# One layer of a pool/S5/ConvFFN decoder on one core: sums and loads queued behind paced instructions, a norm split by tile, pieces of 512 columns

## The chip, the cores and the metric

The kernel runs as one launch on 1 core of a Trainium2 chip. The metric is device time in microseconds, the median of 3 runs. TensorE is called PE here, VectorE DVE, ScalarE ACT, GpSimd POOL, SyncE SP. Each of these engines takes its instructions in the order in which they stand in its own queue; semaphores hold an instruction until the data that it needs, or the buffer that it writes, is there. Everything behind a held instruction on that engine waits too, the DMAs that SP and POOL start among it.

## The reference

2072 tokens (16 meta tokens and 2048 prompt tokens as one sequence, and 8 single sample tokens) pass through one layer of width 1024. Cut to its core:

```python
h = rmsnorm(x, norm1_g)
u_pool, u_ssm, g_pool, g_ssm = split(h @ w_in)            # 512, 512, 1024, 1024 columns
y_pool = pool_mixer(u_pool)                                # windowed means minus the token, then 128 -> 256 per group
y_ssm  = glu_out(ssm_mixer(u_ssm), w_glu)                  # 32 groups, complex diagonal scan
x = x + (sigmoid(g_pool) * y_pool + sigmoid(g_ssm) * y_ssm) @ w_out
h2 = rmsnorm(x, norm2_g)
g, v = split(h2 @ w_up)                                    # 2816 columns each
x = x + (gelu(conv_b + causal_conv3(g, conv_w)) * v) @ w_down
y = rmsnorm(x, norm_f_g)
```

The outputs are y for prompt and sample tokens, and the new pool, SSM and convolution states of both. All is float32.

## The kernel before

**Products.** A float32 operand is split into a high part, rounded by ACT (L126), and a low part, the rest, which DVE (or POOL) subtracts (L127). Each product is three matmuls, high by high, high by low, low by high (`mm3`, L145 to L147).

**First stage, tokens as columns.** The tokens are cut into six `PIECES` of 280, 384, 384, 384, 384 and 256 columns. `norm_piece(j)` loads tiles of 128 tokens (`xt`, four buffers, all by SP), takes the mean square on ACT, the inverse root in a dozen tiny DVE instructions (`rsqrt`, L175 to L186), scales (L260) and transposes on PE (`ptr_n`, L195). Part 0 of the work is pieces 0 and 1, part 1 the others. Eight tiles of `w_in` give u (`pu`, `pp`), then the gates (`pgs`, `pg`, and `py` for the pool map), 24 weight tiles in all, each over every piece: 8 contraction steps of three matmuls a piece. The results go through three buffers tagged `ev` (`us`, `up`, `sg`, `gs`). Before the results of piece 0 are put in, POOL clears a margin of the buffer (L283, L306), and so waits there until the buffer is free.

**Sums of w_up.** `pre_sums` (L325 to L340) prepares sums of blocks of `w_up` for the Strassen-like products below: 22 units, each four POOL-started loads of 128 KB, four POOL instructions, one POOL-started store of 512 KB to `WS`, in two buffers `pre`. They are taken through the loop over the first products, and beside the gates of part 0.

**SSM.** `ssm_setup` builds tables on DVE, which POOL copies (`TSt`, `TCt`, L596, L597); then come the SSM steps, between which gate units of part 1 are put.

**Output product and second norm.** `out_products(j)` multiplies by `w_out` into `po` and adds to x (L1048), tile by tile; `out_norm(j)` does `rsqrt` for all tiles of the piece at once, scales (`xs`, L1066) and transposes (`pn`, L1072), and the result goes to H2 in DRAM.

**Up stage.** Three superblocks s of columns. `b_tiles(s)` loads four tiles of H2 (688 KB each, SP, L1096) and forms four sums: POOL's L1105, L1106, L1123 (L1119 for s > 0), DVE's L1117. Each of the seven operands is split into x. Then 22 steps f, each with seven weight operands made by `w_ops` (loads by SP, high part ACT, low part DVE), each times x in 12 matmuls of 344 columns (`puX`, `puY`, `puZ`). The down product follows (`pd`, 512 columns).

**The order** on each engine is not the program text's: a scheduler with its own time estimates places instructions, within the data dependences and `tc.issue_after`, which keeps an instruction behind another one in the order.

Of the kernel before, what the change touches and what calls it, by code (L numbers as in the profile page):

```python
# [9 lines left out]
F32 = mybir.dt.float32  # L10
F32R = mybir.dt.float32r
# [23 lines left out]

PIECES = [(0, 280), (280, 664), (664, 1048), (1048, 1432), (1432, 1816), (1816, 2072)]
PARTS = [(0, 1), (2, 3, 4, 5)]
SKIP = 14
# [25 lines left out]
def hybrid_kernel(ctx, tc, x_prompt, x_sample, state_pool, state_re, state_im, state_conv, meta,  # L64
# [209 lines left out]
    def u_ssm(m, j, w):  # L274

        a, b = PIECES[j]
        n = b - a
        ps = bank("A", f"pu_{m}_{j}")
        proj(ps, w, j)
        us = evac.tile([P, TC * 50], F32, tag="ev", name=f"us_{m}_{j}", bufs=3)  # L280
        if j == 0:
            u = us.rearrange("p (t c) -> p t c", t=TC)
            GP.memset(u[:, :, 0:16], 0.0)  # L283
            V.tensor_copy(u[:, 7, 0:8], ps[:, 14:22])
            V.tensor_copy(u[:, 0, 8:16], ps[:, 14:22])
# [12 lines left out]
    def u_pool(m, j, w):
# [3 lines left out]
        proj(ps, w, j)  # L302
        up = evac.tile([P, TC * 50], F32, tag="ev", name=f"up_{m}_{j}", bufs=3)
        rows = UP[m * P:(m + 1) * P, :]
        if j == 0:
            GP.memset(up[:, 0:16], 0.0)  # L306
            V.tensor_copy(up[:, 16:30], ps[:, 0:14])
# [8 lines left out]
        else:  # L316
            S.copy(up[:, 0:n], ps[:, 0:n])
            dma(rows[:, 16 + a - 8:16 + b - 8], up[:, 0:n])
            if j == 5:
                pq = bank("B", f"pl_{m}")  # L320
                T.transpose(pq[0:15, 0:P], up[:, n - 15:n], ident)
                V.tensor_copy(psamp[0:15, m * P:(m + 1) * P], pq[0:15, 0:P])
                if m == 3:
                    dma(pool_p[0, 0], psamp[0:15, :])
# [23 lines left out]
    for n, (i, j) in enumerate([(0, 0), (1, 0), (0, 1), (1, 1)] + [(i, j) for i in range(2, 8) for j in PARTS[0]]):  # L348
# [3 lines left out]
        (u_ssm if m >= 4 else u_pool)(m % 4, j, u_w[i])  # L352
        if n in (1, 5, 9, 13):
            norm_piece(2 + n // 4)
        if n >= 6:
            next(pre_units)
    with tc.issue_after(w_ins[0]):
# [36 lines left out]
    def pool_d(g, j):  # L394
# [4 lines left out]
        n = b - a if j else 258  # L399
        ut = gpool.tile([P, 400], F32, tag="ut", name=f"ut_{g}_{j}_{len(hT)}", bufs=2)  # L400
        dma(ut[:, 0:n + 16], UP[g * P:(g + 1) * P, pos0:pos0 + 16 + n])
        cur = ut
        step = 1
        while step < w:
            nxt = gpool.tile([P, 400], F32, tag=f"s{step % 3}", name=f"s_{g}_{j}_{step}", bufs=1)
            lo = 2 * step - 1
            V.tensor_tensor(nxt[:, lo:n + 16], cur[:, lo:n + 16], cur[:, lo - step:n + 16 - step], op=ADD)
            cur = nxt
            step *= 2
        d = gpool.tile([P, 384], F32, tag="d", name=f"d_{g}_{j}", bufs=1)  # L410
        dh = gpool.tile([P, 384], F32R, tag="dh", name=f"dh_{g}_{j}", bufs=2)
        dl = gpool.tile([P, 384], F32R, tag="dl", name=f"dl_{g}_{j}", bufs=2)
        o = 0 if j else NS
# [9 lines left out]
    def gate_pool(g, part):  # L423
# [7 lines left out]
        for j in PARTS[part]:  # L431
# [3 lines left out]
            for i in range(2):  # L435
# [4 lines left out]
                mm3(py[:, 0:n], ph[:, i * P:(i + 1) * P], pl[:, i * P:(i + 1) * P], dh[:, 0:n], dl[:, 0:n], True, True)  # L440
                sg = evac.tile([P, TC * 50], F32, tag="ev", name=f"sg_{m}_{j}", bufs=3)
                S.activation(sg[:, 0:n], ps[:, 0:n], AF.Sigmoid)
# [5 lines left out]
    def gate_ssm(m, part):  # L448
        w = w_in_tile(16 + m, f"gs{part}_{m}")
        for j in PARTS[part]:  # L450
# [4 lines left out]
            proj(ps, w, j, skip)  # L455
            sg = evac.tile([P, TC * 50], F32, tag="ev", name=f"gs_{m}_{j}", bufs=3)
            S.activation(sg[:, 0:n], ps[:, 0:n], AF.Sigmoid)
# [360 lines left out]
    n_steps, done = G + len(STAGES) - 1, 0  # L818
    SSM_END = 68
    units = gate_units()  # L820
# [176 lines left out]
    def out_products(j):  # L997
# [32 lines left out]
        for t, (o, r, p0) in enumerate(tiles):  # L1030
# [19 lines left out]
            jk = osc.tile([P, D], BF16, tag="junk", name=f"ojk_{j}_{t}", bufs=1)  # L1050
            S.activation(jk[0:r], xt[0:r], AF.Square, accum_out=ss[0:r, t:t + 1])
        return ss, rs, x2

    def out_norm(j, ss, rs, x2):
        a = GP_PIECES[j][0]
        tiles = col_tiles(j)
        if j == 0:
            with tc.issue_after(stores[-1]):
# [3 lines left out]
            gdma(H2v[:, :, 0:NU - NG], zpad)  # L1062
        rsqrt(osc, rs[:, 0:len(tiles)], ss[:, 0:len(tiles)], len(tiles), f"n2_{j}")
        for t, (o, r, p0) in enumerate(tiles):
            xs = ost.tile([P, D], F32, tag="xs", name=f"xs_{j}_{t}", bufs=1)
# [19 lines left out]
    asamp = upA.tile([P, NF, NS], F32, name="asamp")  # L1085

    def b_tiles(s):

# [6 lines left out]
        for dst, k0, c in ((b11, 0, c0), (b12, 0, c0 + NH), (b22, 4, c0 + NH), (b21, 4, c0)):  # L1095
            dma(dst, H2v[:, k0:k0 + 4, c:c + NH])  # L1096
        ops = {}
# [9 lines left out]
        if s == 0:  # L1107

            t2 = ot.tile([P, 4 * NH + P], F32, name="t2")[:, P:].rearrange("p (k c) -> p k c", k=4)
            GP.tensor_tensor(t2, b22, t, op=SUB)  # L1110

        def make(key):
            if key in ops:
                return ops[key]
            if key == 6:
                if s:
                    V.tensor_tensor(b11, b22, t, op=SUB)  # L1117
            if key == 4 and s:
                GP.tensor_tensor(b11, b21, b11, op=SUB)  # L1119
            sp(key, {1: b11, 6: b11 if s else t2, 7: b12, 5: t, 3: b22, 4: b11, 2: b21}[key])  # L1120
            return ops[key]

        make.last = lambda: GP.tensor_tensor(b11, b21, t2, op=SUB)  # L1123
        return make
# [3 lines left out]
    def w_ops(s, f):  # L1128
# [4 lines left out]
        st = upA.tile([P, 3, 4, P], F32, tag="st", name=f"ws_{s}_{f}", bufs=2)  # L1133
        later(r1, w_up[:, f * P:(f + 1) * P].rearrange("(k p) c -> p k c", p=P))
        value = w_up[:, DFF + f * P:DFF + (f + 1) * P].rearrange("(k p) c -> p k c", p=P)
        ops = {}

        def sp(key, src):
            if (s, f) == (0, 0) and key in ORDER[:3]:
                hi, lo = [fw0.tile([P, 4, P], F32R, name=f"w{n}0_{key}") for n in "hl"]  # L1140
            else:
                made[0] += 1
                pl, n = (fw, 6) if made[0] % 9 < 6 else (fw2, 3)
                hi = pl.tile([P, 4, P], F32R, tag="wh", name=f"wh{key}_{s}_{f}", bufs=n)
# [180 lines left out]
    lctx = ExitStack()  # L1325
    xc = lctx.enter_context(pool("xc"))
    with tc.high_priority(offset=120):
        for key in ORDER[:3]:
            mk(key)
        mk.last()  # L1330
    pctx.close()
# [273 lines left out]
```

## Time and profile before

| | us |
|---|---|
| median of 3 runs | 2455.31 (2452.75 to 2457.64) |
| profiled execution, whole | 2457.64 |
| its span | 2455.7 |
| PE busy | 2376.1 (97%) |
| DVE busy | 1660.0 (68%) |
| POOL busy | 1036.7 (42%) |
| ACT busy | 983.2 (40%) |

The table is read as follows. The profiled execution is the slowest of the three runs, and 1.9 us of it lie around the span. PE is the engine with next to no slack: 79.6 us of the span are without a matmul. What a change is worth is therefore read from where PE stands idle, and from the length of its queue. The other engines' shares are means over stages that differ much, so the views by stretch are of more use than the means. The stages by time: first norm and u products of part 0 to about 114 us; gates of part 0 to 238; tables of the SSM and u of part 1 to 300; SSM steps with gates to 640; rest of the gates and the GLU to 890; output product and second norm to 1080; up stage to 1990; down stage to the end.

### The profile page before, as it was taken

What the parts mean: (1) busy time and instruction counts of PE and PEld (TensorE: products, weight loads), DVE (VectorE), ACT (ScalarE), POOL (GpSimd) and SP (SyncE); (2) the same over time, 40 slices, a digit from 0 to 9 for tenths busy, and PEclk for the clock granted to TensorE, in tenths of its full rate; (3) what the DMA queues carried; (4) which work ended last, traced back from release to release, by engine and by line L of the source; (5) the groups of instructions that cost most, each with busy time, mean ns of one, the idle gap of its engine ahead of it and who ended that gap; (6) DMA issues with size and microseconds to landing.
All of it is one profiled execution on the core that took longest, in us unless ns stands there. A gap on an engine that the chain in (4) does not pass through costs nothing. (4 is left out here: it accounts for less than half of the span.)

```text
span 2455.7 us, 38129 instructions
## 1 busy us (share of the span) xinstructions
PE 2376.1 (97%) x13628; PEld 2217.1 (90%) x13628; DVE 1660.0 (68%) x2916; ACT 983.2 (40%) x1814; POOL 1036.7 (42%) x1343
## 2 busy tenths in 40 slices
PE   6899999999999999989999999999999999999997
PEld 5899989999999988869999999999999987877876
DVE  6635868997566333468888987778776764555776
ACT  4422222222243122245555655556555543322433
POOL 6676178887113220114565642334333313331373
PEclk9999999999999999999999999999999999999999
DMA  8986543434467576655656665555565577645673
GB/s 250 246 252 205 95 126 104 119 100 116 117 178 222 148 225 192 197 162 169 202 181 203 210 210 182 183 196 170 188 202 172 178 245 265 206 154 168 211 249 125
DMA packets 433137, 449.45 MB, mean 183 GB/s; under 512 B 91372, under 2 KB 349288, under 8 KB 432931
## 3 DMA queue, kind: packets, MB, share of 16 engines
q1 hardware_dynamic: 389091, 353.89, 47.9%
q0 software_dynamic: 18512, 63.48, 7.9%
q10 hardware_dynamic: 25344, 29.66, 3.4%
q8 instruction: 107, 1.75, 0.3%
q14 instruction: 83, 0.68, 0.1%
HBM read 317.38 MB, written 129.86 MB: 182 GB/s over the span
## 5 line engine op out<-in xcount | busy, mean ns | idle before, releaser
L145 PE MATMUL puX<-x,wh 128*128 128x344 f32 x1056 | 337.8, 323 | 6.1 <-ACT u L1201 4.3
L146 PE MATMUL puX<-x,wh 128*128 128x344 f32 x1056 | 339.5, 322 | 1.1 <-DVE x L127 1.1
L147 PE MATMUL puX<-x,wl 128*128 128x344 f32 x1056 | 336.2, 320 | 0.0
L1525 PE MATMUL pd<-th,sl 128*128 128x512 f32 x600 | 235.2, 394 | 4.5 <-DVE sl L127 4.5
L1523 PE MATMUL pd<-th,sh 128*128 128x512 f32 x600 | 234.8, 394 | 3.0 <-ACT th L126 2.0
L1524 PE MATMUL pd<-tl,sh 128*128 128x512 f32 x600 | 236.9, 395 | 0.6 <-DVE tl L127 0.6
L126 ACT CAST wh<-wr 128x512 fp32r<-128x512 f32 x264 | 163.1, 619 | 164.9 <-PE puX L146 99.6
L127 DVE TENSOR_TENSOR wl<-wr,wh 128x512 fp32r<-128x512 f32 x264 | 202.1, 770 | 31.2 <-ACT wh L126 30.8
L1298 POOL TENSOR_TENSOR tr<-tr,tr 128x512 f32<-128x512 f32 x77 | 114.0, 1482 | 243.3 <-DMA tr<-in_w_down_dram 235.7
L127 DVE TENSOR_TENSOR sl<-sr,sh 128x512 fp32r<-128x512 f32 x154 | 133.6, 900 | 121.2 <-ACT sh L126 117.7
L145 PEld LDWEIGHTS puX<-x,wh 128*128 128x128 f32 x1056 | 198.8, 189 | 7.4 <-ACT u L1201 5.2
L127 DVE TENSOR_TENSOR wl<-ws,wh 128x512 fp32r<-128x512 f32 x198 | 168.4, 853 | 52.2 <-ACT wh L126 52.0
L146 PEld LDWEIGHTS puX<-x,wh 128*128 128x128 f32 x1056 | 199.3, 189 | 1.5 <-DVE x L127 1.4
L147 PEld LDWEIGHTS puX<-x,wl 128*128 128x128 f32 x1056 | 199.0, 189 | 0.0
L145 PE MATMUL puZ<-x,wh 128*128 128x344 f32 x528 | 170.3, 323 | 0.0
L146 PE MATMUL puZ<-x,wh 128*128 128x344 f32 x528 | 169.8, 322 | 0.0
L147 PE MATMUL puZ<-x,wl 128*128 128x344 f32 x528 | 168.7, 319 | 0.1
L126 ACT CAST wh<-ws 128x512 fp32r<-128x512 f32 x198 | 122.5, 619 | 109.4 <-PE puX L146 78.2
L126 ACT CAST sh<-sr 128x512 fp32r<-128x512 f32 x154 | 88.1, 617 | 177.9 <-PE pd L1524 159.6
L1523 PEld LDWEIGHTS pd<-th,sh 128*128 128x128 f32 x600 | 113.2, 189 | 31.2 <-ACT th L126 2.5
L1525 PEld LDWEIGHTS pd<-th,sl 128*128 128x128 f32 x600 | 113.1, 189 | 30.8 <-DVE sl L127 5.8
L1524 PEld LDWEIGHTS pd<-tl,sh 128*128 128x128 f32 x600 | 113.3, 189 | 25.6 <-DVE tl L127 1.0
(538 smaller groups left out, 6778.5 us busy)
## 6 DMA issues: line engine op xcount, KB each, us to landing
ws<-WS SPq DMA_DIRECT2D x55, 768.0 KB
wr<-in_w_up_dram SPq DMA_DIRECT2D x77, 512.0 KB
tr<-in_w_down_dram SPq DMA_DIRECT2D x150, 256.0 KB
sr<-SD SPq DMA_DIRECT2D x70, 512.0 KB
SD<-c POOLq DMA_DIRECT2D x44, 344.0 KB, 3.5
wr<-WS SPq DMA_DIRECT2D x55, 256.0 KB
wr<-in_w_up_dram SPq DMA_DIRECT2D x55, 256.0 KB
SD<-e POOLq DMA_DIRECT2D x22, 516.0 KB, 6.8
```

The source lines that it names most:

```text
L126: S.copy(hi, raw)
L127: return (eng or V).tensor_tensor(lo, raw, hi.bitcast(F32), op=SUB)
L145: T.matmul(ps, wh, xh, start=start, stop=False, **kw)
L146: T.matmul(ps, wh, xl, start=False, stop=False, **kw)
L147: T.matmul(ps, wl, xh, start=False, stop=stop, **kw)
L1298: GP.tensor_tensor(raws[0], raws[0], raws[n + 1], op=op)
L1523: T.matmul(acc[j], xh[:, c], th, start=k == 0, stop=False)
L1524: T.matmul(acc[j], xh[:, c], tl, start=False, stop=False)
L1525: T.matmul(acc[j], xl[:, c], th, start=False, stop=k == NP - 1)
```

## The change

There are five parts.

1. The last three pieces of 384, 384 and 256 columns become two of 512. The `ev` buffers and the pool mixer's buffers grow, `d` shares the buffers of the running sums, and gate units of part 1 are spread to step 51 where it was 68, there being fewer of them.
2. A unit of `pre_sums` in the first loop is placed behind the last margin clearing on POOL (`begin[0]`, L283 or L306). The x tiles of later pieces are loaded after n = 1, 5 and 9, pieces of 512 tokens being four tiles.
3. The H2 loads of superblocks 1 and 2 are placed behind the weight load of step f = 12 of the superblock ahead of them (`middle`).
4. `out_norm` takes a range of tiles. The last piece's tile 0 is normed inside `out_products(5)`, tile 1 after the first up products, each with its own `rsqrt` of one column.
5. The pool `fm` is opened earlier, weight operands are shared out 5 and 4 over the two pools where it was 6 and 3, and the sum for key 4 of superblock 0 goes from POOL (`make.last`, L1123) to DVE, at the place where key 4 is made (L1127 after).

```diff
-PIECES = [(0, 280), (280, 664), (664, 1048), (1048, 1432), (1432, 1816), (1816, 2072)]
-PARTS = [(0, 1), (2, 3, 4, 5)]
+PIECES = [(0, 280), (280, 664), (664, 1048), (1048, 1560), (1560, 2072)]
+PARTS = [(0, 1), (2, 3, 4)]
...
-            GP.memset(u[:, :, 0:16], 0.0)
+            begin[0] = GP.memset(u[:, :, 0:16], 0.0).ins
...
-            GP.memset(up[:, 0:16], 0.0)
+            begin[0] = GP.memset(up[:, 0:16], 0.0).ins
...
-        if n in (1, 5, 9, 13):
+        if n in (1, 5, 9):
             norm_piece(2 + n // 4)
         if n >= 6:
-            next(pre_units)
+            with tc.issue_after(begin[0]):
+                next(pre_units)
...
-        d = gpool.tile([P, 384], F32, tag="d", name=f"d_{g}_{j}", bufs=1)
+        d = gpool.tile([P, 528], F32, tag=f"s{step % 3}", name=f"d_{g}_{j}", bufs=1)
...
-    SSM_END = 68
+    SSM_END = 51
...
+            if (j, t) == (5, 0):
+                out_norm(j, ss, rs, x2, (0, 1))
...
-        rsqrt(osc, rs[:, 0:len(tiles)], ss[:, 0:len(tiles)], len(tiles), f"n2_{j}")
-        for t, (o, r, p0) in enumerate(tiles):
+        rsqrt(osc, rs[:, t0:t1], ss[:, t0:t1], t1 - t0, f"n2_{j}_{t0}")
+        for t, (o, r, p0) in list(enumerate(tiles))[t0:t1]:
...
-            dma(dst, H2v[:, k0:k0 + 4, c:c + NH])
+            with tc.issue_after(middle[-1]) if s else nullcontext():
+                dma(dst, H2v[:, k0:k0 + 4, c:c + NH])
...
-            if key == 4 and s:
-                GP.tensor_tensor(b11, b21, b11, op=SUB)
+            if key == 4:
+                (GP if s else V).tensor_tensor(b11, b21, b11 if s else t2, op=SUB)
...
-        make.last = lambda: GP.tensor_tensor(b11, b21, t2, op=SUB)
...
-        later(r1, w_up[:, f * P:(f + 1) * P].rearrange("(k p) c -> p k c", p=P))
+        ins = later(r1, w_up[:, f * P:(f + 1) * P].rearrange("(k p) c -> p k c", p=P)).ins
+        if f == 12:
+            middle.append(ins)
...
-                pl, n = (fw, 6) if made[0] % 9 < 6 else (fw2, 3)
+                pl, n = (fw, 5) if made[0] % 9 < 5 else (fw2, 4)
...
-        mk.last()
...
-    out_norm(5, *rest)
+    out_norm(5, *rest, (1, 2))
```

Three places show how the instructions move. On POOL, at the start of the kernel before (`pre_0`, `pre_1` are the first two units of sums, `us_0` the first buffers to be cleared, `wlo_u` the low parts of the first two weight tiles):

```order
L283 MEMSET us_0_348 128x8x16
L283 MEMSET us_0_382 128x8x16
L334 DMA pre_0_713<-in_w_up_dram 128x2x128
masks.py:199 ISA
masks.py:199 AFFINE_SELECT ident<-ident 128x128
L334 DMA pre_0_713<-in_w_up_dram 128x2x128 x3
L334 DMA pre_1_751<-in_w_up_dram 128x2x128 x4
L127 TENSOR_TENSOR wlo_u_4_234<-raw_u_4_232,whi_u_4_233 128x1024
L335 TENSOR_TENSOR pre_0_713<-pre_0_713 128x256
L127 TENSOR_TENSOR wlo_u_5_240<-raw_u_5_238,whi_u_5_239 128x1024
```

The same place of the changed kernel:

```order
L283 MEMSET us_0_346 128x8x16
L283 MEMSET us_0_380 128x8x16
masks.py:199 ISA
masks.py:199 AFFINE_SELECT ident<-ident 128x128
L127 TENSOR_TENSOR wlo_u_4_232<-raw_u_4_230,whi_u_4_231 128x1024
L127 TENSOR_TENSOR wlo_u_5_238<-raw_u_5_236,whi_u_5_237 128x1024
L283 MEMSET us_0_555 128x8x16
L283 MEMSET us_0_722 128x8x16
L334 DMA pre_0_731<-in_w_up_dram 128x2x128 x4
L334 DMA pre_1_769<-in_w_up_dram 128x2x128 x4
L306 MEMSET up_0_810 128x16
```

The first load of the sums has moved behind the fourth clearing of a buffer; the fourth clearing of an `up` buffer comes 21 rows further on, when three and a half units are through.

On DVE, at the second norm's last piece before (`xs_0` and `xs_1` are its two scaled tiles, `ri_n`, `rt_n`, `ors` belong to its `rsqrt`, `wl` is the low part of a weight operand):

```order
L186 SCALAR_TENSOR_TENSOR ri_n_5_11954<-rt_n_5_11953,ri_n_5_11954 128x2
L1237 SCALAR_TENSOR_TENSOR c_0_12093<-stT,colv,c_0_12093 128x8
L184 TENSOR_TENSOR rt_n_5_11953<-ri_n_5_11954 128x2
L185 TENSOR_TENSOR rt_n_5_11953<-rt_n_5_11953,rh_n_5_11952 128x2
L186 SCALAR_TENSOR_TENSOR ors_11759<-rt_n_5_11953,ri_n_5_11954 128x2
L1066 SCALAR_TENSOR_TENSOR xs_0_11968<-x_5_0_11766,ors_11759,g2B 128x1024
L127 TENSOR_TENSOR wl_0_1_12129<-wr_0_1_11748,wh_0_1_12128 128x512
L127 TENSOR_TENSOR wl_0_2_12255<-wr_0_2_12247,wh_0_2_12254 128x512
L1066 SCALAR_TENSOR_TENSOR xs_1_11984<-x_5_1_11774,ors_11759,g2B 128x1024
```

And in the changed kernel, where the first of the two stands, with the up stage's first operands (`x_0`) behind it and the sum that was POOL's:

```order
L1050 TENSOR_TENSOR x_5_1_10989<-po_1_0_11076,x_5_1_10989 128x512
L1071 SCALAR_TENSOR_TENSOR xs_2_10934<-x_4_2_10773,ors_10695,g2B 128x1024
L1050 TENSOR_TENSOR x_5_1_10989<-po_1_1_11077,x_5_1_10989 128x512
L1071 SCALAR_TENSOR_TENSOR xs_0_11060<-x_5_0_10981,ors_10974,g2B 128x1024
L127 TENSOR_TENSOR x_0_11139<-b_0_10674,x_0_11139 128x1376
L127 TENSOR_TENSOR x_0_11142<-bt_10678,x_0_11142 128x1376
L1127 TENSOR_TENSOR b_0_10674<-b_0_10675,t_10685 128x1376
L127 TENSOR_TENSOR x_0_11152<-b_0_10675,x_0_11152 128x1376
```

`xs_0` has moved ahead of all splits of the first superblock; `xs_1` follows 28 rows after the rows shown.

On SP, the H2 loads of superblock 1 (`b_1`) before, among the last stores to H2 and the weights of step 2 (`wr_0_2`, `ws_2`):

```order
L1049 DMA X2D<-x_5_1_11774 128x1024
L1096 DMA b_1_15367<-H_79 128x4x344
L1096 DMA b_1_15369<-H_79 128x4x344
L995 DMA wr_0_2_12247<-in_w_up_dram 128x8x128
L1096 DMA b_1_15370<-H_79 128x4x344
L1081 DMA H_79<-ht_2_11721 128x8x128
L1096 DMA b_1_15368<-H_79 128x4x344
L995 DMA ws_2_12249<-WS 128x1536
```

And after the change, among the weights of steps 11 to 13:

```order
L997 DMA wr_0_12_13033<-in_w_up_dram 128x8x128
L1104 DMA b_1_14593<-H_79 128x4x344
L997 DMA WS<-ws_11_12881 128x1536
L1104 DMA b_1_14595<-H_79 128x4x344
L997 DMA ws_12_13035<-WS 128x1536
L1104 DMA b_1_14596<-H_79 128x4x344
L1104 DMA b_1_14594<-H_79 128x4x344
L997 DMA wr_0_12_13034<-WS 128x512
```

The four loads have moved ten weight steps down the queue, and POOL's two sums of them with it.

## Rows read from the trace of the kernel before

**Rows 1.** By stretch: PE, PEld, DVE, ACT, POOL busy, clock, DMA, GB/s.

```profile
0.00:24.00 24.00, 5.82 (x27) 4.78 (x28) 13.17 (x42) 10.94 (x20) 15.60 (x23) 1.00 0.78 244
...
65.00:110.00 45.00, 37.40 (x241) 35.99 (x241) 31.09 (x74) 18.54 (x34) 25.25 (x38) 0.92 0.93 244
110.00:235.00 125.00, 124.13 (x836) 123.46 (x835) 62.18 (x100) 37.52 (x67) 88.26 (x115) 1.00 0.77 233
1200.00:1260.00 60.00, 60.00 (x382) 60.00 (x381) 51.11 (x80) 33.01 (x64) 33.72 (x37) 1.00 0.57 178
1380.00:1440.00 60.00, 56.38 (x343) 55.41 (x342) 57.18 (x69) 36.48 (x61) 35.41 (x29) 0.97 0.65 209
420.00:480.00 60.00, 60.00 (x363) 56.22 (x362) 57.99 (x121) 16.72 (x39) 52.25 (x80) 1.00 0.42 119
```

**Rows 2.** Waits of PE, 0 to 120 us: total, times, longest.

```profile
PE ptr_n L195 <- DVE xt L260: 19.2, 5, 11.2
```

**Rows 3.** POOL's DMA queue, 0 to 65 us: packets, MB, share.

```profile
q0 software_dynamic: 1640, 5.02, 26.1%
```

**Rows 4.** Timeline of POOL: start us, us, clearings, stores of the sums, last table.

```profile
65.52 0.21 POOL L283 MEMSET us<- 128x128 f32 x1 [2.77 <-ACT us L295]
...
93.96 0.73 POOL L339 DMA_DIRECT2D WS<-pre  x1 [0.30 <-POOL pre L338]
...
99.28 0.10 POOL L306 MEMSET up<- 128x16 f32 x1
...
240.04 0.79 POOL L339 DMA_DIRECT2D WS<-pre  x1
...
286.30 0.45 POOL L597 COPY TSt<-tb 64x264 f32<-64x264 f32 x1 [6.75 <-DVE tb L593]
```

**Rows 5.** Timeline of PE: runs of 384, 256 and 512 columns.

```profile
689.69 0.33 PE L146 MATMUL pgs<-hTl,whi_gs 128*128 128x384 f32 x1
...
693.15 0.28 PE L145 MATMUL pgs<-hTh,whi_gs 128*128 128x256 f32 x1
...
695.06 0.28 PE L146 MATMUL pgs<-hTl,whi_gs 128*128 128x256 f32 x1
...
974.70 0.39 PE L1044 MATMUL po<-woh,mh 128*128 128x512 f32 x1
...
982.86 0.39 PE L1044 MATMUL po<-woh,mh 128*128 128x512 f32 x1
```

**Rows 6.** Waits of PE, 1070 to 1200 us.

```profile
PE pn L1072 <- DVE xs L1066: 9.0, 1, 9.0
```

**Rows 7.** Timeline of DVE, 1078 to 1108 us.

```profile
1078.67 0.69 DVE L1048 TENSOR_TENSOR x<-po,x 128x512 f32<-128x512 f32 x1 [3.73 <-PE po L1046]
...
1082.28 4.55 DVE L127 TENSOR_TENSOR x<-b,x 128x1376 fp32r<-128x1376 f32 x1
1086.75 1.58 DVE L127 TENSOR_TENSOR x<-t,x 128x1376 fp32r<-128x1376 f32 x1
1088.25 0.68 DVE L127 TENSOR_TENSOR wl<-wr,wh 128x512 fp32r<-128x512 f32 x1
...
1097.18 3.08 DVE L178 TENSOR_SCALAR ri_n<-ri_n 128x2 int32<-128x2 int32 x1
1100.29 0.16 DVE L184 TENSOR_TENSOR rt_n<-ri_n 128x2 f32<-128x2 f32 x1
...
1105.63 1.28 DVE L1066 SCALAR_TENSOR_TENSOR xs<-x,ors,g2B 128x1024 f32<-128x1024 f32 x1
```

**Rows 8.** Timeline of PE after the second transposition of the last piece.

```profile
1115.25 0.40 PE L145 MATMUL puX<-x,wh 128*128 128x344 f32 x1
```

**Rows 9.** Timeline of POOL at the two changes of superblock.

```profile
1080.99 4.38 POOL L1123 TENSOR_TENSOR b<-b,t 128x1376 f32<-128x1376 f32 x1 [62.92 <-issue]
1096.59 3.64 POOL L1105 TENSOR_TENSOR bt<-b,b 128x1376 f32<-128x1376 f32 x1 [11.22 <-DVE x L127]
...
1403.41 3.54 POOL L1105 TENSOR_TENSOR bt<-b,b 128x1376 f32<-128x1376 f32 x1 [2.28 <-DVE x L127]
```

More of the change, by code (lines that the diff above doesn't have):

```diff
@@ L1 @@
 import math
-from contextlib import ExitStack
+from contextlib import ExitStack, nullcontext
 import concourse.bass as bass
@@ L279, in u_ssm @@
         proj(ps, w, j)
-        us = evac.tile([P, TC * 50], F32, tag="ev", name=f"us_{m}_{j}", bufs=3)
+        us = evac.tile([P, TC * 64], F32, tag="ev", name=f"us_{m}_{j}", bufs=3)
         if j == 0:
-            u = us.rearrange("p (t c) -> p t c", t=TC)
-            GP.memset(u[:, :, 0:16], 0.0)
+            u = us[:, 0:TC * 50].rearrange("p (t c) -> p t c", t=TC)
+            begin[0] = GP.memset(u[:, :, 0:16], 0.0).ins
             V.tensor_copy(u[:, 7, 0:8], ps[:, 14:22])
@@ L302, in u_pool @@
         proj(ps, w, j)
-        up = evac.tile([P, TC * 50], F32, tag="ev", name=f"up_{m}_{j}", bufs=3)
+        up = evac.tile([P, TC * 64], F32, tag="ev", name=f"up_{m}_{j}", bufs=3)
         rows = UP[m * P:(m + 1) * P, :]
         if j == 0:
-            GP.memset(up[:, 0:16], 0.0)
+            begin[0] = GP.memset(up[:, 0:16], 0.0).ins
             V.tensor_copy(up[:, 16:30], ps[:, 0:14])
@@ L318, in u_pool @@
             dma(rows[:, 16 + a - 8:16 + b - 8], up[:, 0:n])
-            if j == 5:
+            if j == len(PIECES) - 1:
                 pq = bank("B", f"pl_{m}")
@@ L342, in hybrid_kernel @@
     pre_units = pre_sums()
+    begin = [None]
     norm_piece(0)
@@ L399, in pool_d @@
         n = b - a if j else 258
-        ut = gpool.tile([P, 400], F32, tag="ut", name=f"ut_{g}_{j}_{len(hT)}", bufs=2)
+        ut = gpool.tile([P, 528], F32, tag="ut", name=f"ut_{g}_{j}_{len(hT)}", bufs=2)
         dma(ut[:, 0:n + 16], UP[g * P:(g + 1) * P, pos0:pos0 + 16 + n])
@@ L404, in pool_d @@
         while step < w:
-            nxt = gpool.tile([P, 400], F32, tag=f"s{step % 3}", name=f"s_{g}_{j}_{step}", bufs=1)
+            nxt = gpool.tile([P, 528], F32, tag=f"s{step % 3}", name=f"s_{g}_{j}_{step}", bufs=1)
             lo = 2 * step - 1
@@ L409, in pool_d @@
             step *= 2
-        d = gpool.tile([P, 384], F32, tag="d", name=f"d_{g}_{j}", bufs=1)
-        dh = gpool.tile([P, 384], F32R, tag="dh", name=f"dh_{g}_{j}", bufs=2)
-        dl = gpool.tile([P, 384], F32R, tag="dl", name=f"dl_{g}_{j}", bufs=2)
+        d = gpool.tile([P, 528], F32, tag=f"s{step % 3}", name=f"d_{g}_{j}", bufs=1)
+        dh = gpool.tile([P, 512], F32R, tag="dh", name=f"dh_{g}_{j}", bufs=2)
+        dl = gpool.tile([P, 512], F32R, tag="dl", name=f"dl_{g}_{j}", bufs=2)
         o = 0 if j else NS
@@ L440, in gate_pool @@
                 mm3(py[:, 0:n], ph[:, i * P:(i + 1) * P], pl[:, i * P:(i + 1) * P], dh[:, 0:n], dl[:, 0:n], True, True)
-                sg = evac.tile([P, TC * 50], F32, tag="ev", name=f"sg_{m}_{j}", bufs=3)
+                sg = evac.tile([P, TC * 64], F32, tag="ev", name=f"sg_{m}_{j}", bufs=3)
                 S.activation(sg[:, 0:n], ps[:, 0:n], AF.Sigmoid)
@@ L455, in gate_ssm @@
             proj(ps, w, j, skip)
-            sg = evac.tile([P, TC * 50], F32, tag="ev", name=f"gs_{m}_{j}", bufs=3)
+            sg = evac.tile([P, TC * 64], F32, tag="ev", name=f"gs_{m}_{j}", bufs=3)
             S.activation(sg[:, 0:n], ps[:, 0:n], AF.Sigmoid)
@@ L1051, in out_products, with out_norm @@
             S.activation(jk[0:r], xt[0:r], AF.Square, accum_out=ss[0:r, t:t + 1])
+            if (j, t) == (5, 0):
+                out_norm(j, ss, rs, x2, (0, 1))
         return ss, rs, x2
-    def out_norm(j, ss, rs, x2):
+    def out_norm(j, ss, rs, x2, which=None):
         a = GP_PIECES[j][0]
         tiles = col_tiles(j)
+        t0, t1 = which or (0, len(tiles))
         if j == 0:
@@ L1085, in hybrid_kernel @@
     asamp = upA.tile([P, NF, NS], F32, name="asamp")
+    middle = []
     def b_tiles(s):
@@ L1107, in b_tiles @@
         if s == 0:
-            t2 = ot.tile([P, 4 * NH + P], F32, name="t2")[:, P:].rearrange("p (k c) -> p k c", k=4)
+            t2 = ot.tile([P, 4 * NH + 64], F32, name="t2")[:, 64:].rearrange("p (k c) -> p k c", k=4)
             GP.tensor_tensor(t2, b22, t, op=SUB)
@@ L1326, in hybrid_kernel @@
     xc = lctx.enter_context(pool("xc"))
+    fm = lctx.enter_context(pool("fm"))
     with tc.high_priority(offset=120):
@@ L1344, in hybrid_kernel @@
     fg = lctx.enter_context(pool("fg"))
-    fm = lctx.enter_context(pool("fm"))
     fs = lctx.enter_context(pool("fs"))
```

## The prediction

> **What bounds the kernel now.** I read the busy times by stretch first. From 110 us on PE is without a gap in nearly every stretch: 124.1 of 125 us in the gates, 60.0 of 60 in the SSM steps and in the up stage [rows 1]. Two places fall out: the start, where PE works 5.8 of the first 24 us and 37.4 of the 45 from 65 on, with DMA at 0.78 and 0.93 of its time, and the stretch 1380 to 1440, 56.4 of 60 [rows 1]. Then the waits of PE say what ended the gaps: at the start, 19.2 us of transpositions waited for DVE's scaled x tiles [rows 2]; at the change to the up stage, the last piece's transposition waited 9.0 us for `xs` [rows 6]. The timelines of DVE and POOL there say why `xs` was late, below. The time is thus PE's queue plus these gaps, and each part of the change is priced by one of the two.
>
> **The change part by part.** The sums are made against the profiled execution, 2457.64 us, of which 1.9 lie around the span. It lies 2.3 above the median of 2455.31, so the forecast subtracts the sum from 2457.64 and then 2.3 more.
>
> *Pieces of 512.* A weight tile had 24 matmuls in each of three pieces where it now has 24 in each of two, 24 fewer for each of 24 tiles, and 24 fewer in the pool map. Start to start, 20 matmuls of 384 columns took 3.46 us (689.69 to 693.15), 173.0 ns each; 16 of 256 took 1.91, 119.4 ns; 36 of 512 took 8.16, 226.7 ns [rows 5]. Three pieces cost 2 x 173.0 + 119.4 = 465.4 ns for one contraction step and part, two cost 453.4: 12.0 ns less, times 24 times 24 is 6.9 us, with the pool map's 8 x 3 x 12.0 ns 7.2. Where DVE rather than PE sets the pace nothing comes of it, and in the SSM steps DVE is at 58.0 of 60 us [rows 1]; so 0 to 7.2, and I take 6, since PE is at 60.0 there too. These rows put 13 ns and more above the columns over 2.4 GHz (384 columns: 160.0) into each matmul.
> The Trainium skill (TensorE: Matmul & The Clock Gate, "Wait — 56ns, not 53.3ns?") has matmuls back to back at the columns over 2.4 GHz and about 2.5 ns more. By it 600 fewer matmuls would save an estimated 1.5 us, and the sum below would be 21.5; the trace does not agree with it.
>
> *Sums of w_up at the start.* POOL's queue carried 5.02 MB in the first 65 us, 26.1% of the 16 DMA engines' time, which is 17.0 us [rows 3]. Its first load now stands behind the fourth clearing of an `us` buffer, which ran at 65.5 [rows 4], so nearly all this leaves the time in which x, the gain vector and the first weights are fetched. The gain is at most those 17.0 us (PE is idle 18.2 us of the first 24 and 7.6 from 65 to 110), and at the least a loss of some 3 (the 7% that DMA has free from 65 to 110), because the loads come back between 57 and 100 us, where DMA is at 0.93 already [rows 1], and because a later piece now asks for four tiles at once. I take 8, near the middle: the first stretch's 18.2 us must keep the load of the first tiles and the norm's chain.
>
> The same edit makes the sums late. Before, the seventh unit's store started at 93.96 and the 22nd at 240.04 [rows 4], 9.74 us a unit. In the changed order three and a half units stand before the fourth `up` clearing, which ran at 99.3 [rows 4] and would run near 91; so four units are done by 95 and 18 follow, 175 us, to 270. The last four units stand among the copies of the SSM's tables, whose last ran at 286.3 [rows 4], near 278 with the 8 us. That is tight: a copy now stands behind loads that must land. I take 1.5 us of loss, 0 to 5 at that pace; another pace is the last rival.
>
> *The last piece's norm, and key 4's sum.* Before, from DVE's last addition to x (1078.67) to PE's going on behind the second transposition (1115.25) [rows 7, 8] there are 36.6 us, with 96 matmuls of the up stage in them; after, there are 84. DVE then does, in its order, 7 splits and the sum of 128x1376 at 1.50 us from start to start (1086.75 to 1088.25), 8 low parts at about 0.61 (its 0.68 us overlap alike), two `xs` at 1.2 and some 15 small ones at 0.15 [rows 7]: 12.0 + 4.9 + 2.4 + 2.3 = 21.6, then a us of transposition and 0.6 for the addition, 23.2. The difference of 13.4, less 12 matmuls at 0.157 us (60 us over 382 [rows 1]), leaves 11.5 us. What goes is of two kinds. POOL's key-4 sum from 1080.99 stretched the split beside it to 4.55 us (1.58 is the next one's), and its sums for superblock 1 from 1096.59 stretched an instruction of two columns to 3.08 us (the next took 0.16) [rows 7, 9]. And `xs` of tile 0 stood behind all of it (1105.63). What is late next is again `xs_1`, behind the splits: PE has 84 x 0.157 = 13.2 us of matmuls for those 23.2, so some 8 us of idling stay. From 7, if the splits wait for ACT as well, to 13.4.
>
> *H2 loads of superblocks 1 and 2.* PE lost 3.6 us in 1380 to 1440 [rows 1], where POOL's sums for superblock 2 start at 1403.41 [rows 9] and DVE is at 57.2 of 60. They now fall in the middle of superblock 1. I take 3.5 us gained, 0 to 3.6. The same 2.8 MB and two POOL sums now come at about step 12 of superblocks 0 and 1. The cover is DVE's slack, 8.9 us in 60, and operands made ahead [rows 1]. Two sums held DVE for about 3 us each at 1097; against 8.9 us in 60 that is hidden if the operands are some 6 us ahead. The trace does not show such a sum in mid-superblock. From nothing to 7 us in each of the two (both sums in full and a low part late with them), I take 1.5 in all, close to the covered end, because PE shows 60.0 of 60 there.
> The Trainium skill (SBUF — State Buffer, "Who interferes with whom") says that DVE's second pair of ports is GpSimd's, held by one for a whole instruction while the other is blocked. By that rule the two sums block DVE wherever they stand, and the third rival would follow; the 3.08 us at 1097.18 agree.
>
> *The pools* (`fm`, 5 and 4 for 6 and 3, `d` in the sums' buffers): as many operand buffers as before, nine; hidden by PE's 60.0 of 60, I take nothing, 1 us either way.
>
> The sum: -6 - 8 + 1.5 - 11.5 - 3.5 + 1.5 = -26. 2457.64 - 26 - 2.3 = 2429.3, say 2429 us.
>
> **The rivals.**
> 1. *The start's stall moves and stays.* For it: DMA at 0.93 from 65 to 110, where the loads now go. Against: the larger idle time, 18.2 us, lies in the first 24, which they leave. The gain of 6.5 net is gone: 2436.
> 2. *The pieces give nothing*, because DVE sets the pace where most part-1 projections run. For it: 58.0 of 60 us in the SSM steps. Against: PE at 60.0 there, and larger pieces save DVE instructions too. 6 us less gain: 2435.
> 3. *The stall returns in mid-superblock.* For it: the stretched instructions of rows 7; DVE's low parts are on PE's path. Against: 8.9 us of slack. 7 us in each of two superblocks, where 1.5 is in the sum: 12.5 more, 2441.5.
> 4. *Slower: the sums end too late for the SSM.* The table copies stand behind the last units on POOL, DVE behind the copies, and PE behind the first SSM steps. With gains of 26 us elsewhere and 278 as the time wanted, the loss exceeds the gains from 304 on: (304 - 95) / 18 = 11.6 us a unit. The first seven units took 93.96 / 7 = 13.4 us each; half way, 12.6, ends at 322, 44 late: 2429 + 44 = 2473. For it: POOL takes the start's pace. Against: 9.74 was held while DMA was at 0.77 from 110 to 235 [rows 1], the same stretch in which the 18 now run.
>
> That the pacing does nothing is excluded, since the order shows the first load moved; its price would be rival 1's.
>
> **How the numbers follow.** Forecast 0.55, rival 1 0.16, rival 2 0.08, rival 3 0.15, rival 4 0.06. The bounds that gain most, 17 for 8 at the start and 13.4 for 11.5, together with the pieces' 7.2 reach 2417, and a start better in more than one wait somewhat further: low end 2414. The high end takes in rivals 1 to 3 and two of them together (2436 + 12.5 = 2448): 2448. 0.2%, 4.9 us, is about what a measurement tells from no change. Faster than 2450.4: all but rival 4 and a little of rivals 1 and 3 together, 0.90; within, 0.05; slower 0.05.
>
> **What would show each step.** The stores of the sums: the first after 60 us and the last near 270; PE's wait at the first SSM tables under 6 us. PE's busy time in the first 24 us above 10. Runs of 512 columns at 227 ns in the projections. `xs_1` on DVE some 21 us behind the last x, with no split above 2 us before it. No wait of PE at the changes of superblock, and at about steps 10 to 13 of superblocks 0 and 1 two POOL sums with DVE stretched beside them and PE without gaps. I am wrong if the sums run on beyond 280, or if PE shows several us of gaps in mid-superblock.

## The result, and the profile after

The changed kernel takes 2429.61 us (median of 4 runs, 2426.27 to 2432.80), the kernel before 2454.97 beside it: ratio 0.9896, 95% interval 0.9878 to 0.9914, 25 us less, where 2429 was forecast. The span of its profiled execution is 2431.0 us, 24.7 less than before.

Where the time went is read from when PE starts the same matmul in both traces. A step of the up stage is 84 of its 5544 matmuls.

| start of | before | after | difference |
|---|---|---|---|
| first gate product | 113.7 | 101.0 | -12.7 |
| first SSM product (`pC`) | 306.2 | 299.3 | -6.9 |
| last SSM product (`p`) | 641.5 | 626.6 | -14.9 |
| last w_out product | 1078.2 | 1064.5 | -13.8 |
| up step 9 | 1223.3 | 1196.9 | -26.4 |
| up step 12 | 1263.1 | 1241.7 | -21.4 |
| up step 22 (superblock 1) | 1396.1 | 1375.1 | -20.9 |
| up step 31 | 1521.6 | 1494.5 | -27.1 |
| up step 34 | 1561.5 | 1535.9 | -25.6 |
| last up product | 1991.0 | 1964.8 | -26.2 |
| last down product | 2444.3 | 2419.4 | -24.9 |

Two gains (the start, the change to the up stage), one more at the change of superblock, and two losses, at steps 9 to 12 and 31 to 34. The first row flatters the start: of the 136 transpositions of the first norm, all stood ahead of the first gate product before, and 16 stand behind it now. The last of them starts at 113.7 before and at 104.6 after, 9.1 us earlier. The busy times by stretch of the kernel after (columns as in [rows 1]):

```profile
0.00:24.00 24.00, 7.31 (x34) 6.28 (x35) 16.35 (x51) 13.63 (x23) 6.09 (x10) 1.00 0.80 237
24.00:65.00 41.00, 40.43 (x277) 39.60 (x275) 27.35 (x81) 20.89 (x38) 6.99 (x12) 1.00 0.76 186
65.00:110.00 45.00, 39.45 (x262) 37.27 (x263) 36.09 (x62) 21.45 (x38) 35.21 (x49) 0.96 0.86 259
...
420.00:480.00 60.00, 58.87 (x271) 48.00 (x270) 57.72 (x115) 12.96 (x30) 43.79 (x81) 1.00 0.36 105
1200.00:1260.00 60.00, 56.31 (x346) 55.74 (x345) 54.23 (x74) 29.11 (x57) 39.67 (x38) 0.97 0.67 219
```

Against [rows 1], POOL works 6.1 of the first 24 us in place of 15.6, PE works 40.4 of the 41 us from 24 on, and DMA from 65 to 110 is at 0.86, so the loads that came back fit. PE works 7.3 of the first 24 us where it worked 5.8: a gain of only 1.5, and less than the 10 that the prediction named as a sign. Two stretches that were full are no longer: 420 to 480, and 1200 to 1260. PE's waits from 0 to 120 us (total, times, longest):

```profile
PE ptr_n L195 <- DVE xt L260: 17.6, 6, 9.9
PE ptr_n L195 <- issue: 4.2, 1, 4.2
```

The 19.2 of [rows 2] have hardly shrunk, as most of it is the first wait, in which PE has nothing else. The sums are late, by some 6 us more than reckoned; POOL's last store of one, and the last copy of the SSM's tables:

```profile
275.90 0.72 POOL L339 DMA_DIRECT2D WS<-pre  x1
283.72 0.44 POOL L599 COPY TSt<-tb 64x264 f32<-64x264 f32 x1 [7.10 <-DVE tb L595]
```

270 and 278 were expected, and PE has no wait for the tables. At the change to the up stage, the waits of PE from 1050 to 1200:

```profile
PE pn L1077 <- DVE xs L1071: 3.1, 2, 1.8
```

DVE there has the sum for key 4 at its usual length, and the second `xs` 21.4 us after the last x (1064.90, reckoned: 21.6):

```profile
1064.90 0.69 DVE L1050 TENSOR_TENSOR x<-po,x 128x512 f32<-128x512 f32 x1 [3.73 <-PE po L1048]
...
1069.98 1.58 DVE L1127 TENSOR_TENSOR b<-b,t 128x1376 f32<-128x1376 f32 x1
...
1086.33 1.28 DVE L1071 SCALAR_TENSOR_TENSOR xs<-x,ors,g2B 128x1024 f32<-128x1024 f32 x1
```

The loss in superblock 0 is rival 3, and one of the prediction's two signs of being wrong (several us of gaps in mid-superblock) has come. PE's wait from 1200 to 1400, then POOL, DVE and ACT there:

```profile
PE puX L145 <- ACT m L1210: 3.3, 1, 3.3
```

```profile
1216.26 3.61 POOL L1113 TENSOR_TENSOR bt<-b,b 128x1376 f32<-128x1376 f32 x1
...
1223.15 3.28 POOL L1114 TENSOR_TENSOR b<-b,b 128x1376 f32<-128x1376 f32 x1
```

```profile
1216.78 3.48 DVE L1277 TENSOR_TENSOR e<-c,c 128x344 f32<-128x344 f32 x1
1220.29 0.52 DVE L1278 TENSOR_TENSOR e<-e,c 128x344 f32<-128x344 f32 x1
...
1222.78 4.04 DVE L1280 TENSOR_TENSOR e<-c,e 128x344 f32<-128x344 f32 x1
...
1229.27 0.50 DVE L1220 TENSOR_TENSOR g<-puZ,u 128x344 f32<-128x344 f32 x1
```

```profile
1229.80 0.21 ACT L1228 COPY gsamp<-g 128x8 f32<-128x8 f32 x1 [7.29 <-DVE g L1220]
...
1230.43 0.44 ACT L1210 COPY m<-puX 128x344 f32<-128x344 f32 x1
```

Beside each POOL sum a DVE instruction of 0.5 us takes 3.5 or 4.0. DVE's `g` comes late, ACT's small copy of it waits 7.3 us at the head of ACT's queue, the emptying of `puX` (m) stands behind it, and PE behind that. PE's wait of 3.3 us is not all of the 5.0: in the 5 us behind it, 1231 to 1236, the granted clock is 0.66, part of them at 1.2 GHz where it is 2.4 otherwise, and that is the other 1.7.

### The profile page after: what moved, and what is told of

Read it like the earlier page. It is cut to its first block, busy times and chain, and to the rows that moved or that the text cites. A ratio compares the mean times of both kernels' runs of the same rounds, so it can differ in the third digit from the quotient of the medians.

```text
span 2431.0 us, 36782 instructions
## 1 busy us (share of the span) xinstructions
PE 2365.4 (97%) x13028; PEld 2156.6 (89%) x13028; DVE 1675.1 (69%) x2885; ACT 978.2 (40%) x1786; POOL 1015.2 (42%) x1342
## 4 chain that ended last, share of the span: by engine, by line
PE 79%; DVE 7%; POOL 4%; DMA 4%; issue 3%; ACT 1%; SPq 1%; DVEq 0%; POOLq 0%; ACTq 0%
PE puX L146 6%; PE puX L145 6%; PE puX L147 6%; PE pd L1532 4%; PE pd L1531 4%; PE pd L1533 4%; PE puZ L146 3%; PE puZ L147 3%; PE puZ L145 3%; PE pgs L145 2%; PE po L1046 2%; PE po L1047 2%; PE po L1048 2%; PE pgs L147 2%; PE pgs L146 2%
## 5 line engine op out<-in xcount | busy, mean ns | idle before, releaser
L127 DVE TENSOR_TENSOR wl<-wr,wh 128x512 fp32r<-128x512 f32 x264 | 213.4, 813 | 31.7 <-ACT wh L126 31.4
L127 DVE TENSOR_TENSOR wl<-ws,wh 128x512 fp32r<-128x512 f32 x198 | 158.9, 805 | 45.9 <-ACT wh L126 45.4
L1222 POOL TENSOR_TENSOR v<-u,m 128x344 f32<-128x344 f32 x66 | 80.0, 1212 | 159.8 <-ACT u L1210 159.7
```

The costliest lines, as they stand in the source:

```text
L127: return (eng or V).tensor_tensor(lo, raw, hi.bitcast(F32), op=SUB)
L1222: GP.tensor_tensor(v, u3, m5, op=ADD)
```

## The experiments

Three jobs ran on three chips; in each, the ratio is to the kernel before on the same chip (2463.8, 2463.9, 2461.7 us). The trace of the kernel before is from the job of the result above, in which it ran 7 to 9 us faster, so where a trace and a ratio differ in size, the ratio is the better one. The first of the three jobs has no run of the changed kernel beside it. Traces of one stretch are compared between kernels. In three traces of the changed kernel a stretch of the up stage agrees within 1.3 us, but for steps 31 to 34 (41.1 to 43.5); the stretches ahead of the up stage differ by up to 5 us.

**Undoing one part of the changed kernel.** Pieces of 384 again:

```diff
-PIECES = [(0, 280), (280, 664), (664, 1048), (1048, 1560), (1560, 2072)]
+PIECES = [(0, 280), (280, 664), (664, 1048), (1048, 1432), (1432, 1816), (1816, 2072)]
...
-    SSM_END = 51
+    SSM_END = 68
```

> The changed kernel with pieces of 384, 384 and 256 columns and step 68 put back, all else as changed. Theory (PE's queue sets the time, 12.0 ns for each of 576 contraction steps and part): about 7 us slower than the changed kernel's 2429.6, so 2436.5, and all of it lies between the first SSM products and the first w_out product; the start up to the first gates and everything behind 1065 us keep their lengths. Rival (DVE sets the pace beside the SSM steps): within 1.5 us of 2429.6.

0.9898 (0.9885 to 0.9912), 2438.9 us. From the first SSM product to the first w_out product it takes 567.4 us, as the changed kernel does: the place was wrong. It is late before that, by 8 us; PE's wait from 125 to 330, and POOL's last sums:

```profile
PE pC L697 <- DMA crow_CA<-in_ssm_C_re_dram: 7.8, 1, 7.8
```

```profile
283.21 1.45 POOL L339 DMA_DIRECT2D WS<-pre  x2
```

In this order the last two units are stored 7 us later than in the changed kernel. SP starts the loads of `crow_CA` (the SSM's C, which `pC` reads) at 302.4, there at 292.3. It looks as if the late sums held the loads, but the kernel before speaks against it: its sums end at 240.0 and its loads start at 302.1 all the same. SP's loads of `crow_CA` in the kernel before, in this one, and in the changed one (durations in ns, first and last start):

```profile
L693 SPq DMA_DIRECT2D crow_CA<-in_ssm_C_re_dram x8: 422/438/1413, 302.1 to 309.3; - x8
```

```profile
L695 SPq DMA_DIRECT2D crow_CA<-in_ssm_C_re_dram x8: 382/430/1494, 302.4 to 310.1; - x8
```

```profile
L695 SPq DMA_DIRECT2D crow_CA<-in_ssm_C_re_dram x8: 383/430/665, 292.3 to 300.1; - x8
```

In the three kernels with pieces of 384 that were traced they start at 301.5 to 302.4, whether the sums end at 240 or at 284; in the eleven traces with pieces of 512, at 292.3 to 297.8, whether the sums end at 241 or at 279. So the pieces set this time: the loads stand on SP among the stores of u, 24 of them with pieces of 384 and 20 with 512. What holds those stores is not taken apart.

The early sums unpaced:

```diff
-            with tc.issue_after(begin[0]):
-                next(pre_units)
+            next(pre_units)
```

> The changed kernel without the pacing of the early sums; its first loads stand on POOL at the kernel's start again. Theory (5 MB of loads and POOL's additions in the first 65 us delay x, the gain vector and the first norm): the first gates start 11 to 13 us later (at 101.0 in the changed kernel), the first SSM tables' products about 7 us later, because the sums end some 30 us earlier and no longer hold the tables up: 2436.5 in all. Rival (the stall only moves to the later pieces): first gates within 3 us, 2431.

0.9939 (0.9925 to 0.9952), 2447.5 us. The first gates start at 111.3 in place of 101.0, the last SSM product at 638.6 in place of 626.6. The theory's mechanism holds at the gates (10.3 us later; 11 to 13 expected), but the first SSM product comes only 2.9 later where 7 were expected: the rest of the loss shows behind it, because PE does fewer of part 1's products ahead of it (26 matmuls of `pp` where the changed kernel has 52). The total is 11 us over the theory's.

The H2 loads unpaced:

```diff
-            with tc.issue_after(middle[-1]) if s else nullcontext():
+            if True:
                 dma(dst, H2v[:, k0:k0 + 4, c:c + NH])
```

> The changed kernel without the pacing of superblock 1's and 2's H2 loads, so that POOL's two sums stand at the change of superblock again. Theory (POOL's sums hold DVE wherever they stand): 4 us more at the change to the up stage, 5.0 us less at steps 9 to 12 of superblock 0, 1.4 less in superblock 1, 6.2 more at the change to superblock 1: 3.8 in all, 2433.4. Rival (the gain at the change to the up stage is the split norm's alone): nothing there, so -0.2, 2429.4.

0.9911 (0.9897 to 0.9924), 2441.1 us. From the last w_out product to step 9: 140.8 us, where the changed kernel takes 132.4 and the one before 145.0; steps 9 to 12: 39.8, where the changed kernel takes 44.9; steps 22 to 31: 125.7 against 119.3; steps 31 to 34: 39.8 against 41.4. The losses of the changed kernel in mid-superblock are gone, and the changes to the up stage and to superblock 1 have theirs back: 8.4 us at the first, where the theory had 4, and 6.4 at the second. PE's wait from 1060 to 1200 and, from DVE, two instructions of eight columns beside POOL's sums:

```profile
PE pn L1077 <- DVE xs L1071: 8.6, 2, 7.4
```

```profile
1082.05 2.97 DVE L1245 TENSOR_SCALAR c<-stT,colv 128x8 f32<-128x8 f32 x1
...
1085.06 3.12 DVE L1246 SCALAR_TENSOR_TENSOR c<-stT,colv,c 128x8 f32<-128x8 f32 x1
```

In the changed kernel the same two take 0.28 and 0.23 us. The 5.6 us more are all of the lateness of the second `xs`, which comes 27.0 us behind the last x here and 21.4 there.

The last norm whole:

```diff
-            if (j, t) == (5, 0):
-                out_norm(j, ss, rs, x2, (0, 1))
...
-    out_norm(5, *rest, (1, 2))
+    out_norm(5, *rest)
```

> The changed kernel with the last piece's norm done for both tiles at once behind the first up products, as before. Theory (POOL's sums, now gone from there, were most of the stall, and the second tile's norm is behind the same splits with or without the first): the second tile's scaling waits for the first one's transposition, 3 us more at the change to the up stage, 2432.6. Rival (the split norm is the whole gain of 13.0 us there): 11 to 13 us more, 2441.

0.9924 (0.9912 to 0.9937), 2443.3 us. From the last w_out product to step 9: 135.6, 3.2 us more than the changed kernel, as the theory had it; the split norm is a quarter of the gain there. The total, however, is nearer the rival's 2441: steps 9 to 12 take 47.3, 2.5 more, and 3.5 us lie ahead of the norm, in the same instructions, and are not explained.

**The control, the pieces alone, and POOL's sums one by one.**

> The changed kernel itself, as the control for the runs beside it: 0.9896 of the kernel before, and the same stretches as in its first trace (first SSM products at 299.3, first w_out product at 866.7, 1088.5 behind the last transposition) within 3 us.

0.9871 (0.9857 to 0.9885), 2430.2 us; its stretches as expected but for the last, 1084.7, 3.8 us earlier. The ratio is below the 0.9896 expected: the changed kernel repeats its time, and the kernel before is the slower one here.

The kernel before with this alone (the buffers of 400, 384 and 50 columns grow with it, as in the change):

```diff
-PIECES = [..., (1048, 1432), (1432, 1816), (1816, 2072)]
+PIECES = [..., (1048, 1560), (1560, 2072)]
...
-    SSM_END = 68
+    SSM_END = 51
```

> The kernel before with pieces of 512 and step 51 alone. Theory (PE's queue sets the time, 7.2 us less in it): 0.9971 of the kernel before, all of it between 163 us and the first w_out product, and PE idle no longer than before there. Rival (what PE saves is lost to waits on DVE and POOL in the SSM steps and the GLU, as from the first SSM product to the first w_out product of the changed kernel with pieces of 384 and of 512, 567.4 us each): 0.9995 to 1.000, with new waits of PE for POOL's gc and for the GLU's splits.

0.9979 (0.9970 to 0.9988): 5.2 us less (3.0 to 7.4). Against the trace of before the first gates are 5.1 us earlier, but the last transposition of the first norm only 0.8: the same 16 transpositions have moved behind the gate. The first SSM product is 6.9 earlier, the first w_out product 4.9: what is gained is there at the start of the SSM steps, and nothing is added after it. SP starts the loads of `crow_CA` at 294.8 where it was 302.1, and PE's waits for them are 0.3 us where they were 4.1. PE's waits from 330 to 1050 were 5.4 us in all before and are 11.8 here (5.4 to 6.1 in three kernels with pieces of 384, 10.6 to 12.7 in seven traces with 512), the longest new ones:

```profile
PE pyo L794 <- POOL gc L785: 5.2, 3, 3.0
...
PE pglu L145 <- ACT whi_glu L126: 2.3, 1, 2.3
```

The changed kernel has the same ones:

```profile
PE pyo L796 <- POOL gc L787: 4.3, 5, 1.5
...
PE pglu L145 <- ACT whi_glu L126: 1.8, 1, 1.8
PE pglu L147 <- DVE wlo_glu L127: 1.5, 1, 1.5
```

The total is near the theory's; the waits are the rival's, and they took back the gain behind the first SSM product. Neither held whole.

Key 4's sum on POOL, started early:

```diff
-            if key == 4:
-                (GP if s else V).tensor_tensor(b11, b21, b11 if s else t2, op=SUB)
+            if key == 4 and s:
+                GP.tensor_tensor(b11, b21, b11, op=SUB)
...
+        mk.last()
```

> The changed kernel with key 4's sum of superblock 0 on POOL again, early (a 128x1376 subtraction of 4.4 us). Theory (POOL's sums hold DVE): a split beside it takes 4.5 us where 1.6 is usual, and the change to the up stage is 2 to 4 us longer than the control's; the rest as the control: 0.9908. Rival (that sum was hidden): within 1 us of the control.

0.9888 (0.9873 to 0.9903), 2435.9 us. POOL's sum, and the split beside it on DVE:

```profile
1068.23 4.37 POOL L1131 TENSOR_TENSOR b<-b,t 128x1376 f32<-128x1376 f32 x1 [64.17 <-issue]
```

```profile
1069.51 4.53 DVE L127 TENSOR_TENSOR x<-b,x 128x1376 fp32r<-128x1376 f32 x1
```

From the last w_out product to step 1 it takes 26.2 us, the control 24.0, to step 9 133.3 against 131.9: 1.4 to 2.2 us, at or below the low end of the theory. The total is 4 us over the control's by the ratios, but the intervals overlap.

The two sums of superblocks 1 and 2 on DVE:

```diff
+        E = V if s else GP
-        GP.tensor_tensor(t, b12, b11, op=SUB)
-        GP.tensor_tensor(b12, b22, b12, op=SUB)
+        E.tensor_tensor(t, b12, b11, op=SUB)
+        E.tensor_tensor(b12, b22, b12, op=SUB)
```

> The changed kernel with the two sums of superblocks 1 and 2 (bt and b12) on DVE in place of POOL. Theory (the 5.0 us lost at steps 9 to 12 of superblock 0 and the 1.4 in superblock 1 come from POOL's sums holding DVE for 3.5 us each, where DVE needs 1.5 for the same sum): DVE is occupied for 3.0 us a pair in place of 7, the stall of 3.4 us goes, and 4 to 6 us are gained: 0.9876. Rival (the 2.8 MB of H2 loads ahead of weights are what stalls there): no gain, 0.9896.

0.9867 (0.9852 to 0.9882), 2429.6 us. Steps 9 to 12 take 39.8, the control 46.0; steps 31 to 34 39.8 against 43.5. The H2 loads stand where they stood, so the sums' engine is the cause of both losses. The sums on DVE:

```profile
1218.62 1.58 DVE L1114 TENSOR_TENSOR bt<-b,b 128x1376 f32<-128x1376 f32 x1
...
1223.46 1.57 DVE L1115 TENSOR_TENSOR b<-b,b 128x1376 f32<-128x1376 f32 x1
```

The total shows nothing of it in this job. In the trace, the GLU and the output product took 5.3 us more than the control's, with the same instructions.

**The third job.** The kernel before with the pacing of the sums alone:

```diff
-            GP.memset(u[:, :, 0:16], 0.0)
+            begin[0] = GP.memset(u[:, :, 0:16], 0.0).ins
...
-            next(pre_units)
+            with tc.issue_after(begin[0]):
+                next(pre_units)
```

> The kernel before with the pacing of the early sums alone. Theory (the sums' loads and additions cost the start 8 to 11 us, and their lateness costs nothing, PE doing 5.4 us more of part 1's products ahead of the SSM tables): first gates near 103, the last SSM product 9 to 11 us earlier than in the kernel before (641.5), 0.9960 in all. Rival (their lateness takes part of it back, as PE's wait of 7.8 us for crow_CA in the changed kernel with pieces of 384 has it): first gates near 103 all the same, but the last SSM product only 1 to 4 us earlier, with several us of waits for crow_CA, 0.9990.

0.9950 (0.9936 to 0.9963): 12.3 us less. In its trace the first gates start at 102.5, the last transposition at 104.4 (113.7 before), and the last SSM product 6.9 us earlier than before; between, PE's wait from 125 to 330, here and in the kernel before:

```profile
PE pC L697 <- DMA crow_CA<-in_ssm_C_re_dram: 6.3, 1, 6.3
```

```profile
PE pC L695 <- DMA crow_CA<-in_ssm_C_re_dram: 4.1, 3, 1.4
```

Theory's total, rival's wait: the start gives 9 us in the same work. That the sums' lateness takes a part back is not shown: the kernel before, without it, waits 4.1 us for the same loads, which start at 302.1 there and at 301.5 here. PE reaches them earlier and waits longer.

The H2 loads early and their sums on DVE (both edits above):

> The changed kernel with superblock 1's and 2's H2 loads unpaced and their two sums on DVE. Theory (it is POOL's holding of DVE that cost 6.3 us at the change to the up stage and 6.4 at the change to superblock 1; DVE alone needs 3.0 a pair): 3 us or less at either place, up stage no longer than the changed kernel's. Rival (the loads stand ahead of weights and are what stalls): 6 us at both places as with the sums on POOL.

0.9890 (0.9875 to 0.9905), 2436.0 us. Steps 22 to 31 take 119.4, as in the changed kernel: there POOL's sums were all. But from the last w_out product to step 9 it takes 141.9, no less than with the sums on POOL. The second `xs` comes 28.3 us behind the last x, where the changed kernel has 21.4: 3.0 us are DVE's two sums, and 3.4 its wait for a high part from ACT, which waited for weights. What ACT waited for, and SP's queue:

```profile
1093.54 0.62 ACT L126 CAST wh<-wr 128x512 fp32r<-128x512 f32 x1 [7.88 <-DMA wr<-WS]
```

```profile
1080.88 4.43 SPq L1104 DMA_DIRECT2D b<-H  x1
1085.40 0.94 SPq L997 DMA_DIRECT2D ws<-WS  x1
```

The fourth H2 load is held 4.4 us on SP, and the weights of the next step stand behind it. So the loads cost by themselves there too; how much without either sum, no run shows. The rival came at the first place and the theory at the second.

The two sums on DVE once more, with the edit as above:

> The changed kernel with the two sums of superblocks 1 and 2 on DVE, again. In its first trace steps 9 to 34 of the up stage took 334.3 us where the control had 341.6, but its median was the control's, its GLU and output product having taken 5.3 us more than the control's with the same instructions. Theory (that was chance): 3 to 7 us below the control's median. Rival (something in this program makes the middle stages longer): the same median again, and again long stretches there.

0.9863 (0.9848 to 0.9878), 2428.1 us. Steps 9 to 34 take 334.4, its control 339.4, and the median is 5.1 us below the control's, as the theory had it.

That control:

> The changed kernel itself, as the control for the runs beside it: 0.987 to 0.990 of the kernel before.

0.9885 (0.9868 to 0.9903), 2433.2 us. Over both jobs the version with DVE's sums has a median of 2429.3 us in 8 runs, the changed kernel 2432.2 in 8: the stretch gains 5 to 7 us in the traces, and the total is unclear, the intervals overlapping.

## Why the prediction was right

The total was met within a us, by mechanisms that were mostly there and by terms that missed in both directions. That it fits so closely is luck: the start gave 6 us more than reckoned and the middle of the superblocks lost 5 us more, and in the two jobs with a control the change is worth 32 and 28 us.

- *The start, -8 and +1.5.* Too small: 12.3 us alone (9.1 to 15.8 by the interval), where 6.5 net was reckoned, and 10 us at the gates in the run that undoes it. The lateness was forecast within 6 us (275.9 for 270, 283.7 for 278), and in the changed kernel costs PE no wait. With pieces of 384 PE waits 6.3 and 7.8 us for `crow_CA`, but 4.1 in the kernel before too, and these loads start at the same time with early and with late sums. So no run shows the loss of 1.5, nor rival 4. (Half way between rival 4's 11.6 and 13.4 is 12.5, not 12.6, which makes its price 42 us.) Of the working, PE's first 24 us gave 1.5, not the 4 that the sign of 10 us asked for; most of the gain lies from 24 to 110.
- *Pieces, -6.* The size holds (-5.2), the step does not. "PE is at 60.0 there too" was taken to mean that a shorter queue is a shorter time. It was not: some 6 of the 7.2 us lie behind the first SSM product, and there they came back as 6.4 us of waits, nearly all for POOL and DVE, which is rival 2. The gain came ahead of the SSM steps, where the loads of `crow_CA` start 7 to 10 us earlier with pieces of 512; that way is not in the prediction, so the size is luck. How the 6.9 us there divide between these waits and PE's shorter queue is not separated.
- *The change to the up stage, -11.5.* 12.6, from the last w_out product to step 9. By the prediction's own measure, from DVE's last addition to PE's going on (1064.90 to 1088.53), it is 23.6 us where 23.2 was reckoned. ("Some 8 us of idling" does not follow from that working, 23.2 less 13.2 being 10; PE's idle time there is 5.9.) The step named POOL's sums and the place of `xs`; what the text did not have is a third cause, the H2 loads on SP ahead of the weights. Loads and sums together are 8.4 us; with the loads early, taking the sums off POOL gave nothing back there, as DVE then does them in that place and waits for weights. The split norm gives 3, key 4's sum 1 to 2.
- *H2 loads.* -3.5 at the change to superblock 1 was 6.2: PE's idle time counted 3.6, but the matmuls at the lower clock after the stall (0.97 in that row) were left out. The row had the answer: 343 matmuls where a full 60 us has 382, 39 at 0.157 us, are 6.1. +1.5 for the middle of superblocks 0 and 1 was 5.0 and 1.6 (up to 6.4 and 3.7 in the controls). This is the step that failed: "hidden if the operands are some 6 us ahead". PE's wait names no operand: what was late was the emptying of PSUM, behind DVE's `g` and ACT's small copy. Rival 3 came, within its price of 7 us a superblock.
- The rest of the way, 1.1 us at the GLU and output product and 1.4 in the down stage, is no larger than what one program shows from run to run.

So -14.9 (reckoned -12.5), +1.1, -12.6, +5.0 and 0.5, -6.2, +1.6, and 0.7 to the end make -24.8 in the spans, with -26 reckoned. The Trainium skill's rule on the shared ports (SBUF — State Buffer, "Who interferes with whom"), which was put to rival 3, agrees with the 2.97 to 4.53 us of DVE's instructions beside POOL's sums in these runs.

## What to carry to other kernels

An engine busy for 60 of 60 us need not be the only bound if another one is at 58: shorten its queue, and waits can appear. Before a wait is put down to what came late, look whether the kernel without the lateness has it too. A moved instruction takes its harm along: ask at the new place what stands behind each engine it slows, the emptying of PSUM and the head of ACT's queue as well as the operands. And where two engines hold each other up, as POOL's sums and DVE do here, the engine that does the work in 1.5 us can be the better place, rather than the idle one that needs 3.5 and holds the other: here that took 5 to 7 us off a stretch, with the total unclear.

## What was not expected of the hardware

The same program repeats the up stage's undisturbed steps to 0.1 us (39.8 for three steps in five kernels), but the GLU and output product, from the first GLU product to the last w_out product, took 385.6, 380.7 and 384.3 us in three traces of the changed kernel. The start varies as well: in nine traces of kernels in which PE does the same up to there, the first gate product starts at 101.0 to 106.3. And the kernel before was at 2455 us in the job of the result and at 2462 to 2464 in the other three, while the changed one stayed at 2430 to 2433, so that its ratio ranges from 0.9871 to 0.9896.
